# Second MLP products by Strassen's algorithm in three of four blocks, and a token order made at the output projection

## The chip, the cores and the metric

The kernel runs on one core of a Trainium2 chip (trn2). The metric is device time in microseconds for one execution, lower is better. The engines are named as in the profile: PE (TensorE matmul), PEld (its weight load), DVE (VectorE), ACT (ScalarE), POOL (GpSimd) and SP (SyncE, which issues most DMAs).

## The reference

A trunk of two residual layers over 1024 tokens of width 1024 in float32: neighbourhood attention and an MLP, then a gated DeltaNet and an MLP, and a last norm. The change is in the MLPs and in the output projection ahead of the first:

```python
def sq_relu_mlp(h, w1, w2):
    a = jax.nn.relu(h @ w1)
    return (a * a) @ w2

for i in range(DEPTH):          # DEPTH = 2, D_FF = 4096
    m, j = i % N_MIXERS, i // N_MIXERS
    if m == 0:
        h = h + neighbourhood_attention(rmsnorm(h, na_norm[j]), na_w_qkv[j], na_rpb[j], na_w_o[j])
    elif m == 1:
        h = h + gated_deltanet(rmsnorm(h, gdn_norm[j]), gdn_w_in[j], gdn_conv[j], ...)
    h = h + sq_relu_mlp(rmsnorm(h, mlp_norm[i]), mlp_w1[i], mlp_w2[i]).astype(h.dtype)
return rmsnorm(h, final_norm)
```

## The kernel before

Activations are held transposed: 8 row tiles d of 128 features by 1024 tokens, in two halves of 512 tokens. Each float32 operand is split into a high part (cast to fp32r on ACT, tiles `whi` and the like) and a low part (the difference, on DVE, `wlo`), and a product is three matmuls of 128x512: high x high, high x low, low x high (line 157).

`block` (line 91) runs an output projection and an MLP. `out_gather` (line 282) multiplies the attention result with `wo`, adds the residual `hr` at the eviction (line 305), takes squares and sums them over d on POOL (line 189), writes the residual to DRAM (`hs`), and gathers the seven right operands of Strassen's algorithm for the first products. The halves come in the order (d, 0), (d, 1); with `order` 2 the last four are (6, 0), (7, 0), (6, 1), (7, 1).

`mlp_first` (line 326) computes the hidden layer by Strassen's algorithm (Winograd's form): 16 column groups n, each with seven products of 12 matmuls (line 363). POOL forms the four left sums `s` (line 338) and two of the additions (line 348), ACT and DVE split the left operands (lines 353, 354), DVE evicts (line 348), scales and clips (line 343), ACT squares, and SP writes the result to DRAM (`hidden`).

`mlp_second` (line 400) multiplies the hidden layer with `w2` the plain way: four blocks b of 1024 hidden features; in each, for d and half, 24 matmuls into one PSUM bank, and one DVE addition to the residual `h` (line 431). The eight operand pairs of a block come from DRAM as tiles of 128x1024 and are split by `hidden_tile` (lines 394 to 396), those of the first block beside the last column group of `mlp_first` (`late`), those of the next beside the running one. `unspill` (line 709) loads the whole residual ahead of the first block. In the first MLP the last block reorders tokens from rows of the grid to the order that the next layer wants: with `reorder` the right operand of each matmul is read through a strided view, and the eviction goes to a new tile `hn` (line 428). After the last block `after` takes the norm of the result.

No planner sets the order of this part: each engine runs its instructions in the order that the tile framework lays down from the program, and tiles with a tag and `bufs` (three of `whi` and `wlo`, two of `mm`) say how far one engine may run ahead.

## Time and profile before

| | |
|---|---|
| median of 3 runs | 2812.89 us (2808.34 to 2814.01) |
| the profiled execution: its time | 2804.47 us |
| its span, granted TensorE clock | 2802.7 us, 0.985 |
| PE, DVE, ACT, POOL busy | 96%, 57%, 39%, 27% |
| first products of the first and second MLP, from and to | about 600 to 923 us, about 2090 to 2405 us |
| second products of the first and second MLP | about 925 to 1295 us, about 2410 to 2800 us |

Busy time is the time in which an engine works on an instruction. A matmul's end is modelled, so what one costs is read from how many start in a stretch. "Idle before" is the engine's idle time ahead of an instruction, with what ended it. The granted clock is a share of full speed.

### The profile page before, as it was taken

The numbers are of one execution on the slowest core, as the hardware profiler recorded it, in microseconds if no ns is written. First come the engines' busy times: TensorE is split into PE (matmuls) and PEld (weight loads), VectorE is DVE, ScalarE is ACT, GpSimd is POOL, SyncE is SP. The second block draws the span as 40 slices with busy tenths as digits, with TensorE's granted clock in tenths as the row PEclk, the third lists the DMA queues.
The fourth block names the chain that finished last, engine by engine and source line by source line (L and its number), as shares of the span: only waits on it lengthen the run. The fifth ranks groups of instructions, "written<-read, shape, count | busy, mean of one in ns | idle before, by whom it ended". The sixth has DMA issues, their size and how long they took to land. (4 is left out here: it accounts for less than half of the span.)

```text
span 2802.7 us, 39699 instructions
## 1 busy us (share of the span) xinstructions
PE 2704.1 (96%) x14460; PEld 2137.0 (76%) x14460; DVE 1603.9 (57%) x3137; ACT 1101.9 (39%) x2375; POOL 765.1 (27%) x951
## 2 busy tenths in 40 slices
PE   8999999999999999999998999999979999899998
PEld 6766666678888788887777887787858888788887
DVE  5155555665555532334778887787595555633333
ACT  5144444443333321123454555455353333411224
POOL 0111111154444000011334555543164444100001
PEclk9999999999999999999999999999989999999999
DMA  7212212333432532222221222214363433521323
GB/s 192 55 50 50 58 46 52 124 116 114 151 105 91 193 109 85 68 83 81 49 48 41 48 52 54 50 35 125 110 189 100 144 113 102 199 90 61 109 69 116
DMA packets 311667, 261.05 MB, mean 93 GB/s; under 512 B 78127, under 2 KB 256943, under 8 KB 311471
## 3 DMA queue, kind: packets, MB, share of 16 engines
q1 hardware_dynamic: 303054, 250.03, 29.8%
q0 software_dynamic: 3072, 8.39, 1.3%
q8 instruction: 114, 1.87, 0.3%
q10 hardware_dynamic: 5344, 0.09, 0.1%
q14 instruction: 83, 0.67, 0.1%
HBM read 183.56 MB, written 66.49 MB: 89 GB/s over the span
## 5 line engine op out<-in xcount | busy, mean ns | idle before, releaser
L157 PE MATMUL mm<-X,whi 128*128 128x512 f32 x1792 | 579.1, 399 | 5.9 <-ACT whi L133 5.0
L1371 PE MATMUL mm<-A,whi 128*128 128x512 f32 x1216 | 405.5, 414 | 1.1 <-DVE A L1371 1.1
L157 PEld LDWEIGHTS mm<-X,whi 128*128 128x128 f32 x1792 | 335.3, 188 | 87.6 <-issue 7.5
L157 PE MATMUL mm<-A,whi 128*128 128x512 f32 (+1 forms) x1104 | 350.5, 397 | 15.4 <-DVE hr L305 7.0
L157 PE MATMUL mm<-X,wlo 128*128 128x512 f32 x896 | 356.8, 399 | 0.0
L133 ACT CAST whi<-wraw 128x512 fp32r<-128x512 f32 (+1 forms) x210 | 128.0, 612 | 475.8 <-PE mm L157 427.1
L189 POOL TENSOR_TENSOR rs<-rs,r 128x512 f32<-128x512 f32 x55 | 77.5, 1410 | 797.2 <-ACT r L188 797.1
L157 PEld LDWEIGHTS mm<-A,whi 128*128 128x128 f32 x1104 | 207.2, 189 | 68.7 <-DVE hr L305 8.1
L1371 PEld LDWEIGHTS mm<-A,whi 128*128 128x128 f32 x1216 | 215.6, 191 | 41.5 <-DVE A L1371 1.9
L1371 PE MATMUL mm<-A,wlo 128*128 128x512 f32 x608 | 242.2, 398 | 0.0
L134 DVE TENSOR_TENSOR wlo<-wraw,whi 128x512 fp32r<-128x512 f32 (+1 forms) x210 | 155.1, 741 | 128.5 <-ACT whi L133 128.0
L431 DVE TENSOR_TENSOR h<-mm,h 128x512 f32<-128x512 f32 x111 | 76.7, 691 | 248.1 <-PE mm L157 247.6
L157 PE MATMUL mm<-A,wlo 128*128 128x512 f32 (+1 forms) x552 | 217.7, 395 | 0.1
L157 PEld LDWEIGHTS mm<-X,wlo 128*128 128x128 f32 x896 | 168.7, 188 | 37.6 <-issue 1.7
L344 ACT ACTIVATE r<-r 128x512 f32<-128x512 f32 x128 | 80.9, 632 | 234.2 <-DVE r L343 234.2
L354 DVE TENSOR_TENSOR wlo<-s,whi 128x512 fp32r<-128x512 f32 x128 | 118.8, 928 | 88.4 <-ACT whi L353 88.3
L1371 POOL TENSOR_TENSOR xt<-lp,xi 128x126 f32<-128x126 f32 (+22 forms) x248 | 106.0, 427 | 175.8 <-DMA lp<-dsc 157.0
L1371 DVE SCALAR_TENSOR_TENSOR X<-xp,cw,X 128x512 f32<-128x512 f32 x192 | 143.4, 788 | 1.7 <-ACT X L1371 1.0
L1371 PEld LDWEIGHTS mm<-A,wlo 128*128 128x128 f32 x608 | 115.5, 190 | 28.0
L157 PEld LDWEIGHTS mm<-A,wlo 128*128 128x128 f32 x552 | 104.7, 190 | 24.4 <-DVE wlo L134 0.5
L1371 POOL TENSOR_TENSOR xi<-xi,xt 128x126 f32<-128x126 f32 (+22 forms) x248 | 116.6, 470 | 19.4
L353 ACT CAST whi<-s 128x512 fp32r<-128x512 f32 x128 | 78.5, 613 | 76.2 <-PE mm L363 50.3
(331 smaller groups left out, 5346.5 us busy)
## 6 DMA issues: line engine op xcount, KB each, us to landing
wraw<-in_mlp_w_dram SPq DMA_DIRECT2D x148, 256.0 KB
quad<-in_mlp_w_dram SPq DMA_DIRECT2D x64, 512.0 KB
hidden<-r SPq DMA_DIRECT2D x128, 256.0 KB
X<-hidden SPq DMA_DIRECT2D x32, 512.0 KB
A<-hidden SPq DMA_DIRECT2D x32, 512.0 KB
wraw<-in_gdn_w_in_dram SPq DMA_DIRECT2D x64, 256.0 KB
wraw<-in_na_w_qkv_dram SPq DMA_DIRECT2D x32, 256.0 KB
hr<-hs SPq DMA_DIRECT2D x32, 256.0 KB
```

The source lines that it names most:

```text
L133: nc.scalar.copy(out=hi[:, :nk], in_=raw[:, :nk])
L134: nc.vector.tensor_tensor(out=lo[:, :nk], in0=raw[:, :nk], in1=hi[:, :nk].bitcast(FP32), op=ALU.subtract)
L157: nc.tensor.matmul(out=ps, lhsT=a, rhs=b, start=n == 0, stop=n == last)
L189: nc.gpsimd.tensor_tensor(out=st["acc", half], in0=st["acc", half], in1=sq, op=ALU.add)
L344: nc.scalar.activation(out=t, in_=t, func=AF.Square)
L353: nc.scalar.copy(out=hi, in_=left[j])
L354: nc.vector.tensor_tensor(out=lo, in0=left[j], in1=hi.bitcast(FP32), op=ALU.subtract)
L431: nc.vector.tensor_tensor(out=hv, in0=ps, in1=hv, op=ALU.add)
L1371: r = f(*args, **kw)
```

## The change

The second products of blocks 0 to 2 go by Strassen's algorithm too. A new class `Second` holds them: for each block b the seven products j in the order 1, 5, 2, 6, 3, 7, 4 (seven phases), and in each phase the four column groups q, each 12 matmuls into one of four PSUM banks. The right operands are quarter tiles of the hidden layer (128x512) and sums of them, the left ones quarters of `w2` and sums. POOL makes both kinds of sums in place (`combine`, `difference`) one to four phases ahead, ACT and DVE split the right operand of the next phase beside the running one (`split`), and the products are added up in the residual `h` and in three accumulators z, y, w. In the third block the eight whole tiles for the fourth block are loaded and split (`load`, `whole`), and POOL adds the accumulators to `h`. The first block's loads, splits and differences stand in the last column groups of `mlp_first` (`prepare`). The fourth block stays plain. `unspill` is gone; halves of the residual are loaded where they are first needed. Tokens of the first MLP are reordered at the eviction of the output projection: the sum goes through a strided view into a tile `now` of 128x1024, and square, spill and gather of both halves follow the second half; the last four halves there come as (6, 0), (6, 1), (7, 0), (7, 1).

```diff
-    def block(self, name, group, rest, spare, y, wo, gain, early, order, w1, w2, after, **how):
+    def block(self, name, group, rest, free, spare, y, wo, gain, early, order, w1, w2, after, moved=False, **how):
         st, other = {}, "X" if group == "A" else "A"
-        a = []
-
-        def late(j):
-            for f in {1: (0,), 5: (1, 2), 2: (3,), 6: (4, 5), 3: (6,), 7: (7,)}.get(j, ()):
-                a.append(self.hidden_tile(group, 0, f))
-
+        second = Second(self, group, other, rest, free, w2)
         with self.phase(name + "a", 1):
             get = self.operands(group, rest)
             with self.inner(name + "h"):
-                todo = self.out_gather(y, wo, gain, st, get, spare, early, order)
+                todo = self.out_gather(y, wo, gain, st, get, spare, early, order, moved)
             with self.inner(name + "w"):
-                self.mlp_first(st, w1, get, other, todo, late)
+                self.mlp_first(st, w1, get, other, todo, second, moved)
         with self.phase(name + "b"):
-            self.unspill()
-            self.mlp_second(a, (group, other), w2, after, **how)
+            a, h = second.blocks()
+            self.mlp_second(a, h, w2, after, **how)
...
-    def out_gather(self, y, wo, gain, st, get, spare, early, tail):
+    def out_gather(self, y, wo, gain, st, get, spare, early, tail, moved):
...
-        for n, (d, half) in enumerate(self.sequence(tail)):
+        for d, half in self.sequence(tail):
             if d not in w:
                 w = w if len(y) < 4 else {}
                 w[d] = self.weight(wo[:, d * P:(d + 1) * P])
-            hv = self.wk2.tile([P, HALF], FP32, tag="hr", name=self.uid("hr"), bufs=5)
-            nc.sync.dma_start(out=hv, in_=old[d][:, half * HALF:(half + 1) * HALF])
+            was = self.half("r") if moved else self.wk2.tile([P, HALF], FP32, tag="hr", name=self.uid("hr"), bufs=5)
+            nc.sync.dma_start(out=was, in_=old[d][:, half * HALF:(half + 1) * HALF])
             ps = self.product(w[d], y, half)
-            nc.vector.tensor_tensor(out=hv, in0=ps, in1=hv, op=ALU.add)
-            self.sumsq(d, half, hv, st)
-            self.spill(d, hv, half)
-            self.gather(d, half, hv, gain, get, raw, late)
-            if d // 2 < early:
-                for j in (5, 6, 7, 4):
-                    for f in late.pop(j, ()):
-                        f()
+            if moved:
+                if half == 0:
+                    now = self.wk2.tile([P, S], FP32, tag="hr", name=self.uid("hr"), bufs=2)
+                view = lambda t: t.rearrange("p (t r c) -> p t r c", r=16, c=8)
+                nc.vector.tensor_tensor(out=now.rearrange("p (r t c) -> p t r c", t=8, c=8)[:, 4 * half:4 * half + 4],
+                                        in0=view(ps), in1=view(was), op=ALU.add)
+                there = [(k, now[:, k * HALF:(k + 1) * HALF]) for k in range(2)] if half else []
+            else:
+                nc.vector.tensor_tensor(out=was, in0=ps, in1=was, op=ALU.add)
+                there = [(half, was)]
+            for k, hv in there:
+                self.sumsq(d, k, hv, st)
+                self.spill(d, hv, k)
+                self.gather(d, k, hv, gain, get, raw, late)
+                if d // 2 < early:
+                    for j in (5, 6, 7, 4):
+                        for f in late.pop(j, ()):
+                            f()
...
-                if n == nq - 1:
-                    late(j)
-
...
+                second.prepare(n - nq, j)
...
+    def combine(self, j, q):
+
+        tr = self.tr
+        if j == 5:
+            self.s[q] = tr.work("s1", [P, 4, P], 4)
+            self.less(self.s[q], self.left(7, q), self.left(4, q), ALU.add)
+        elif j == 6:
+            self.less(self.s[q], self.s[q], self.left(1, q))
+        elif j == 7:
+            self.less(self.left(7, q), self.left(7, q), self.left(1, q))
+        else:
+            self.less(self.left(2, q), self.left(2, q), self.s[q])
...
+    def prepare(self, n, j):
...
+        if j == 1:
+            for i in range(3):
+                self.split(0, 0, i)
+            self.load_b(0, "12", 0)
+        elif j == 5:
+            self.split(0, 0, 3)
+            self.load_b(0, "12", 1)
+        elif j == 2:
+            for i in range(4):
+                self.difference(5, i)
+            self.load_b(0, "21", 0)
+            self.load_w(0, 1, 0)
...
+    def beside(self, b, pos, q):
+
+        last = b == self.nb - 1
+        if pos < 6:
+            self.split(b, pos + 1, q)
+        elif not last:
+            self.split(b + 1, 0, q)
+        if pos == 0:
+            self.combine(5, q)
+        elif pos == 1:
+            self.combine(6, q)
+            self.difference(6, q)
+        elif pos == 2:
+            self.difference(7, q)
+        elif pos == 3:
+            self.combine(3, q)
+            self.difference(4, q)
+        elif pos == 4:
+            self.combine(7, q)
+        if not last:
+            if pos in (2, 3) and q % 2:
+                self.load_w(b + 1, 0, 2 * (pos - 2) + q // 2)
+            elif pos == 4:
+                self.load_b(b + 1, ("11", "22")[q // 2], q % 2)
+            elif pos == 5 and q % 2:
+                self.load_b(b + 1, "12", q // 2)
+            elif pos == 6:
+                self.difference(5, q)
+                self.load_w(b + 1, 1, q)
+                if q % 2:
+                    self.load_b(b + 1, "21", q // 2)
+        else:
+            n = 4 * pos + q
...
+            z, y, w = [self.sums[t, q] for t in "zyw"]
+            add = lambda out, x: self.less(out, out, x, ALU.add)
+            if pos == 5:
+                add(y, z)
+                add(self.h[2 * q, 1], y)
+            elif pos == 6:
+                add(self.h[2 * q + 1, 0], z)
+                add(self.h[2 * q + 1, 0], w)
+                add(w, y)
+                t = self.tr.work("h22", [P, HALF], 2)
+                self.tr.nc.sync.dma_start(out=t, in_=self.tr.hs[2 * q + 1][:, HALF:])
+                add(w, t)
+                self.h[2 * q + 1, 1] = w
...
+    def blocks(self):
...
+        for q in range(4):
+            fetch(2 * q, 0)
+        for b in range(self.nb):
+            self.block = b
+            for pos, j in enumerate(tr.ORDER):
+                for q in range(4):
+                    if b == 0 and pos in (2, 4):
+                        fetch(2 * q + pos // 4, 1 - pos // 4)
+                    hi, lo = [tr.sb.tile([P, 4, P], F32R, tag=tag, name=tr.uid(tag), bufs=3) for tag in ("whi", "wlo")]
+                    w = self.left(j, q)
+                    nc.scalar.copy(out=hi, in_=w)
+                    nc.vector.tensor_tensor(out=lo, in0=w, in1=hi.bitcast(FP32), op=ALU.subtract)
+                    ps = tr.ps.tile([P, HALF], FP32, tag="mm", name=tr.uid("mm"), bufs=2) if m % 2 else tr.bank("pq", [P, HALF], 2)
+                    m += 1
+                    for i in range(4):
+                        x = self.ops[j, i]
+                        for n, (u, v) in enumerate(((hi, 0), (hi, HALF), (lo, 0))):
+                            nc.tensor.matmul(out=ps, lhsT=u[:, i], rhs=x[:, v:v + HALF], start=i == 0 and n == 0, stop=i == 3 and n == 2)
+                    z, y, w = [self.sums[t, q] for t in "zyw"]
+                    if j in (1, 2):
+                        add(self.h[2 * q, 0], ps)
+                    elif j in (3, 4):
+                        add(self.h[2 * q, 1] if j == 3 else self.h[2 * q + 1, 0], ps)
+                    elif j == 6:
+                        add(z, ps)
+                    elif b:
+                        add({5: y, 7: w}[j], ps)
+                    else:
+                        nc.scalar.copy(out={5: y, 7: w}[j], in_=ps)
+                    if j == 1:
+                        if b:
+                            r = tr.half("r")
+                            nc.scalar.copy(out=r, in_=ps)
+                            self.less(z, z, r, ALU.add)
+                        else:
+                            nc.scalar.copy(out=z, in_=ps)
+                    self.beside(b, pos, q)
+        return self.ready, lambda d, half: self.h[d, half]
...
-    t.block("mlp0", "A", [f"X{i}" for i in range(7)], None, y, a["na_w_o"][0], g_m0, 3, 2, a["mlp_w1"][0], a["mlp_w2"][0], after, reorder=True)
+    t.block("mlp0", "A", [f"X{i}" for i in range(7)], [f"X{i}" for i in range(8, 14)], None, y, a["na_w_o"][0], g_m0, 3, 0,
+            a["mlp_w1"][0], a["mlp_w2"][0], after, moved=True)
```

How the order of instructions moves is shown at three places. DVE in the second block of the first MLP's second products, before (`mm` is a PSUM bank, `h2` to `h4` the residual, `wlo` a weight's low part):

```order
L134 TENSOR_TENSOR wlo_2153_8768<-wraw_2151_8765,whi_2152_8767 128x512
L431 TENSOR_TENSOR h2_2112_8540<-mm_2147_8733,h2_2112_8540 128x512
L134 TENSOR_TENSOR wlo_2160_8831<-wraw_2158_8828,whi_2159_8830 128x512
L431 TENSOR_TENSOR h3_2113_8542<-mm_2154_8771,h3_2113_8542 128x512
L134 TENSOR_TENSOR wlo_2163_8837<-wraw_2161_8834,whi_2162_8836 128x512
```

Between two weight splits stands one eviction, and a product of 24 matmuls belongs to each. After, in the third and fourth phase of the first block (`A0` to `A9`, `A2` are split right operands, `X4` and `X15` their sources, `A6` and `A7` the accumulator z, `mm` and `pq` PSUM banks):

```order
L242 TENSOR_TENSOR A0_2181_8856<-X4_2100_8476,A0_2181_8856 128x512
L242 TENSOR_TENSOR A8_2185_8879<-X4_2100_8476,A8_2185_8879 128x512
L242 TENSOR_TENSOR A1_2190_8904<-X15_2101_8479,A1_2190_8904 128x512
L1501 TENSOR_TENSOR h60_2119_8548<-mm_2175_8818,h60_2119_8548 128x512
L1514 TENSOR_TENSOR wlo_2188_8887<-s1_2134_8620,whi_2187_8886 128x512
L242 TENSOR_TENSOR A9_2194_8927<-X15_2101_8479,A9_2194_8927 128x512
L1501 TENSOR_TENSOR A6_2110_8536<-pq_2180_8842,A6_2110_8536 128x512
L1514 TENSOR_TENSOR wlo_2192_8910<-s1_2139_8644,whi_2191_8909 128x512
L1501 TENSOR_TENSOR A6_2110_8536<-mm_2184_8865,A6_2110_8536 128x512
L1514 TENSOR_TENSOR wlo_2198_8937<-A4_2087_8423,whi_2197_8936 128x512
L1501 TENSOR_TENSOR A7_2111_8537<-pq_2189_8890,A7_2111_8537 128x512
L1514 TENSOR_TENSOR wlo_2204_8964<-A12_2093_8447,whi_2203_8963 128x512
```

Twelve DVE operations now belong to four products of 12 matmuls, eight of them with both inputs in SBUF, and three operand splits stand together ahead of an eviction.

POOL from the end of the first MLP's first products, before (`r` is a hidden tile, `rs0` and `rs1` the sums of squares for the next layer's norm):

```order
L348 TENSOR_TENSOR r_2097_8466<-r_2097_8466,X15_2089_8437 128x512
L348 TENSOR_TENSOR r_2103_8495<-X14_2075_8381,X7_2069_8357 128x512
L189 TENSOR_TENSOR rs0_2368_10251<-rs0_2368_10251,r2_2383_10330 128x512
L189 TENSOR_TENSOR rs1_2372_10284<-rs1_2372_10284,r2_2386_10363 128x512
L189 TENSOR_TENSOR rs0_2368_10251<-rs0_2368_10251,r2_2397_10410 128x512
```

After, POOL's first operations for the second block (`s1` a weight sum from the two halves of the weights `X5` and `A4`, `X12`, `X13`, `X0` and `X1` quarter tiles of the hidden layer):

```order
L1359 TENSOR_TENSOR s1_2265_9258<-X5_2166_8786,A4_2242_9154 128x512
L1359 TENSOR_TENSOR X12_2201_8958<-X0_2228_9084,X12_2201_8958 128x512
L1359 TENSOR_TENSOR X5_2166_8786<-X5_2166_8786 128x4x128
L1359 TENSOR_TENSOR X12_2201_8958<-X0_2228_9084,X12_2201_8958 128x512
L1359 TENSOR_TENSOR X13_2207_8985<-X1_2237_9129,X13_2207_8985 128x512
L1359 TENSOR_TENSOR X0_2228_9084<-X0_2228_9084,X4_2213_9012 128x512
L1359 TENSOR_TENSOR s1_2271_9284<-X6_2177_8836,A12_2247_9178 128x512
L1359 TENSOR_TENSOR X0_2228_9084<-X0_2228_9084,X4_2213_9012 128x512
L1359 TENSOR_TENSOR X13_2207_8985<-X1_2237_9129,X13_2207_8985 128x512
```

POOL had nothing between the last addition of the first products and the sums of squares in the fourth block. Now 124 operations stand there in each MLP, and the first of a block (`s1`) stands ahead of the differences for that block's second phase (`X12`, `X13`).

POOL at the end of the first MLP's output projection, before (`raw` is a gathered operand, `rcol` the scales):

```order
L189 TENSOR_TENSOR rs0_1396_5193<-rs0_1396_5193,r2_1513_5790 128x512
L189 TENSOR_TENSOR rs1_1402_5230<-rs1_1402_5230,r2_1524_5839 128x512
L189 TENSOR_TENSOR rs1_1402_5230<-rs1_1402_5230,r2_1534_5885 128x512
L276 TENSOR_TENSOR raw_1503_5745<-raw_1503_5745,raw_1536_5892 128x512
L276 TENSOR_TENSOR raw_1514_5794<-raw_1514_5794,raw_1536_5892 128x512
L195 TENSOR_TENSOR rcol_1555_5959<-rcol_1555_5959,mhalf_70 128x4
```

After:

```order
L180 TENSOR_TENSOR rs1_1403_5231<-rs1_1403_5231,r2_1514_5785 128x512
L180 TENSOR_TENSOR rs0_1399_5222<-rs0_1399_5222,r2_1527_5860 128x512
L267 TENSOR_TENSOR raw_1512_5780<-raw_1512_5780,raw_1532_5876 128x512
L180 TENSOR_TENSOR rs1_1403_5231<-rs1_1403_5231,r2_1530_5869 128x512
L186 TENSOR_TENSOR rcol_1551_5943<-rcol_1551_5943,mhalf_70 128x4
L267 TENSOR_TENSOR raw_1528_5864<-raw_1528_5864,raw_1532_5876 128x512
```

The squares of tile 7 (`r2_1527`, `r2_1530`) are both added after the last product, with a difference between them.

## Rows read from the trace of the kernel before

**Rows 1.** The page's first part: busy time, share and instructions of each engine.

```profile
PE 2704.1 (96%) x14460; PEld 2137.0 (76%) x14460; DVE 1603.9 (57%) x3137; ACT 1101.9 (39%) x2375; POOL 765.1 (27%) x951
```

**Rows 2.** Stretches: length, busy time (instructions) of PE, PEld, DVE, ACT, POOL; clock, DMA share, GB/s.

```profile
620.00:900.00 280.00, 280.00 (x1205) 225.26 (x1204) 161.10 (x228) 107.57 (x187) 128.26 (x88) 1.00 0.36 115
965.00:1215.00 250.00, 250.00 (x1074) 201.43 (x1073) 78.57 (x106) 45.14 (x63) 0.00 (x0) 1.00 0.26 81
1222.00:1282.00 60.00, 60.00 (x266) 49.53 (x265) 25.00 (x37) 22.44 (x36) 14.63 (x11) 1.00 0.34 105
```

**Rows 3.** Groups, 640 to 900 us (last: 960 to 1200): count, busy, mean ns, idle before.

```profile
L354 DVE TENSOR_TENSOR wlo<-s,whi 128x512 fp32r<-128x512 f32 x55 | 51.0, 927 | 37.9 <-ACT whi L353 37.9
L354 DVE TENSOR_TENSOR wlo<-quad,whi 128x512 fp32r<-128x512 f32 x39 | 26.7, 685 | 7.9 <-ACT whi L353 7.9
L348 DVE TENSOR_TENSOR r<-pq,X 128x512 f32<-128x512 f32 x26 | 17.8, 686 | 19.5 <-PE pq L363 19.5
...
L353 ACT CAST whi<-s 128x512 fp32r<-128x512 f32 x54 | 33.1, 613 | 31.0 <-PE mm L363 23.7 <-PE p L363 7.3
...
L338 POOL TENSOR_TENSOR s<-quad 128x512 f32<-128x512 f32 x14 | 23.5, 1676 | 16.8 <-DVE wlo L354 16.8
L338 POOL TENSOR_TENSOR s<-s,quad 128x512 f32<-128x512 f32 x14 | 18.1, 1295 | 47.4 <-DVE wlo L354 47.4
...
L396 DVE TENSOR_TENSOR A<-A,A 128x1024 fp32r<-128x1024 f32 x8 | 9.7, 1222 | 4.4 <-ACT A L395 4.4
```

**Rows 4.** Timeline in the first MLP's first products: start, length, engine, instruction.

```profile
750.97 1.29 POOL L348 TENSOR_TENSOR r<-X,X 128x512 f32<-128x512 f32 x1 [1.41 <-DVE X L348]
751.50 1.31 DVE L354 TENSOR_TENSOR wlo<-s,whi 128x512 fp32r<-128x512 f32 x1 [0.61 <-ACT whi L353]
...
741.53 0.69 DVE L348 TENSOR_TENSOR r<-mm,X 128x512 f32<-128x512 f32 x1 [1.27 <-PE mm L363]
742.14 0.68 DVE L354 TENSOR_TENSOR wlo<-s,whi 128x512 fp32r<-128x512 f32 x1
...
612.79 1.25 POOL L338 TENSOR_TENSOR s<-quad,quad 128x512 f32<-128x512 f32 x1
614.01 1.26 POOL L338 TENSOR_TENSOR s<-quad 128x512 f32<-128x512 f32 x1
```

**Rows 5.** Timeline where both engines have work queued, second MLP's output projection.

```profile
2081.57 1.78 DVE L251 TENSOR_TENSOR A<-raw,A 128x512 fp32r<-128x512 f32 x1
2083.27 1.78 DVE L254 SCALAR_TENSOR_TENSOR X<-hr,g_m,X 128x512 fp32r<-128x512 f32 x1
...
2081.05 1.75 POOL L189 TENSOR_TENSOR rs<-rs,r 128x512 f32<-128x512 f32 x1
2082.75 1.75 POOL L276 TENSOR_TENSOR A<-A,A 128x512 f32<-128x512 f32 x1
```

**Rows 6.** Stretches at the change from first to second products, both MLPs.

```profile
920.00:940.00 20.00, 16.56 (x63) 12.46 (x62) 19.90 (x23) 14.09 (x18) 3.23 (x2) 0.91 0.57 201
940.00:960.00 20.00, 18.32 (x79) 14.41 (x78) 9.27 (x12) 3.53 (x5) 0.00 (x0) 1.00 0.88 295
2400.00:2420.00 20.00, 15.60 (x53) 11.57 (x53) 17.39 (x20) 15.06 (x20) 2.32 (x2) 0.83 0.54 180
2420.00:2440.00 20.00, 17.70 (x76) 13.91 (x74) 10.26 (x12) 3.86 (x6) 0.90 (x1) 1.00 0.99 347
2440.00:2460.00 20.00, 19.50 (x78) 15.70 (x79) 9.74 (x13) 5.56 (x8) 0.00 (x0) 0.91 0.30 94
```

**Rows 7.** PE's waits for the sums of squares: total us, times, longest.

```profile
PE pa L203 <- POOL rs L189: 6.2, 2, 5.4
```

**Rows 8.** Stretches in the gated DeltaNet, columns as in rows 2.

```profile
1360.00:1380.00 20.00, 16.89 (x74) 13.49 (x74) 16.65 (x42) 10.08 (x29) 6.18 (x8) 0.83 0.14 27
1440.00:1460.00 20.00, 18.38 (x119) 15.83 (x118) 16.09 (x45) 13.18 (x39) 2.77 (x6) 1.00 0.07 11
```

**Rows 9.** A stretch at the end of the second MLP's output projection.

```profile
2080.00:2100.00 20.00, 12.38 (x50) 10.28 (x49) 18.59 (x19) 9.00 (x16) 18.01 (x12) 0.67 0.27 84
```

More of the change, by code (lines that the diff above doesn't have):

```diff
@@ L142, in pair, with product @@
         return self.slot(f"{group}{i}", F32R), self.slot(f"{group}{8 + i}", F32R)
-    def product(self, w, xs, half, order=None, sl=None, ps=None):
+    def product(self, w, xs, half, sl=None):
         nc = self.nc
-        ps = ps or self.ps.tile([P, HALF], FP32, tag="mm", name=self.uid("mm"), bufs=2)
+        ps = self.ps.tile([P, HALF], FP32, tag="mm", name=self.uid("mm"), bufs=2)
         sl = sl or slice(half * HALF, (half + 1) * HALF)
@@ L151, in product @@
         for (whi, wlo), (xhi, xlo) in zip(w, xs):
-            if order is None:
-                hi, lo = xhi[:, sl], xlo[:, sl]
-            else:
-                hi, lo = order(xhi)[:, 8 * half:8 * half + 8], order(xlo)[:, 8 * half:8 * half + 8]
-            for a, b in ((whi, hi), (whi, lo), (wlo, hi)):
-                nc.tensor.matmul(out=ps, lhsT=a, rhs=b, start=n == 0, stop=n == last)
+            for a, b in ((whi, xhi), (whi, xlo), (wlo, xhi)):
+                nc.tensor.matmul(out=ps, lhsT=a, rhs=b[:, sl], start=n == 0, stop=n == last)
                 n += 1
@@ L386, in mlp_first, with mlp_second @@
                     finish(add(self.half("r2"), ps, p1), 1, 0)
-                if n == nq - 1:
-                    late(j)
-    def hidden_tile(self, group, b, f):
+                second.prepare(n - nq, j)
+    def mlp_second(self, a, h, w2, after, tail=2, cut=False):
         nc = self.nc
-        hi, lo = self.pair(group, f)
-        nc.sync.dma_start(out=lo.bitcast(FP32), in_=self.hidden[b * ND + f])
-        nc.scalar.copy(out=hi, in_=lo.bitcast(FP32))
-        nc.vector.tensor_tensor(out=lo, in0=lo.bitcast(FP32), in1=hi.bitcast(FP32), op=ALU.subtract)
-        return hi, lo
@@ new lines, in mlp_second @@
+        w = [None, None]
+        for d, half in self.sequence(tail):
+            if w[0] != d:
+                w = [d, self.weight(w2[w2.shape[0] - D:, d * P:(d + 1) * P])]
+            hv = h(d, half)
+            if cut and (d, half) == (ND - 1, 1):
+                for part in range(2):
+                    sl = slice(part * 256, part * 256 + 256)
+                    ps = self.product(w[1], a, half, sl=slice(HALF + sl.start, HALF + sl.stop))
+                    nc.vector.tensor_tensor(out=hv[:, sl], in0=ps, in1=hv[:, sl], op=ALU.add)
+                    after(d, half, hv[:, sl], part)
+                continue
+            ps = self.product(w[1], a, half)
+            nc.vector.tensor_tensor(out=hv, in0=ps, in1=hv, op=ALU.add)
+            after(d, half, hv)
@@ L689, in na @@
         return y + [y7]
-    def out_proj(self, y, wo, after, tail=2):
-        nc = self.nc
-        w = {}
-        for i, (d, half) in enumerate(self.sequence(tail)):
-            if d not in w:
-                w = w if len(y) < 4 else {}
-                w[d] = self.weight(wo[:, d * P:(d + 1) * P])
-            ps = self.product(w[d], y, half, ps=self.bank("pa", [P, HALF]) if i == 2 else None)
-            hv = self.h[d][:, half * HALF:(half + 1) * HALF]
-            nc.vector.tensor_tensor(out=hv, in0=ps, in1=hv, op=ALU.add)
-            after(d, half, hv)
     def spill(self, d, hv, half=None):
@@ L707, in spill @@
         self.nc.sync.dma_start(out=dst, in_=hv)
-    def unspill(self):
-        self.h = []
-        for d in range(ND):
-            h = self.work(f"h{d}")
-            self.nc.sync.dma_start(out=h, in_=self.hs[d])
-            self.h.append(h)
     def gdn_consts(self, conv, onorm):
```

133 lines of the change are left out of this document (95 added, 38 removed).

## The prediction

> **What bounds the kernel now.** I read the busy shares first: TensorE (PE) is busy for 96% of the span, VectorE (DVE) for 57%, GpSimd (POOL) for 27% [rows 1]. So the end is set by PE's instruction stream, and an edit pays by the matmuls it removes, as long as the others can still feed PE. Then I read the stretches of the MLPs. In the first products 1205 matmuls start in 280 us, 0.2324 us each; in the second products 1074 in 250 us, 0.2328 us; both at granted clock 1.00 [rows 2]. PE does not wait there. In the second products DVE works 79 of 250 us and POOL not at all; in the first products, already Strassen, DVE works 161 of 280 us and POOL 128 [rows 2]. The change turns the first picture into something heavier than the second, so the question is what DVE and POOL cost each other.
>
> They do cost each other. The same DVE subtraction (wlo) takes 685 ns beside no POOL work and 927 ns on average where POOL writes its input; POOL's own addition takes 1295 or 1676 ns [rows 3]. One case is plain: POOL's addition starts at 750.97 and lasts 1.29 us, and the DVE subtraction that starts at 751.50 ends at 752.81, 0.55 us after POOL's end. Undisturbed, DVE starts an operation each 0.61 us (741.53, 742.14) and POOL each 1.22 (612.79, 614.01) [rows 4]. With both queued they go in lockstep: DVE starts at 2081.57 and 2083.27, POOL at 2081.05 and 2082.75, so 1.70 us buy one of each, about 1.25 for POOL and 0.45 for DVE [rows 5]. DVE's additions from PSUM have one input in SBUF; they keep 686 ns [rows 3].
>
> **The change: matmuls.** Each Strassen block has 7 x 4 products of 12 matmuls, 336 where 384 stood. Three blocks in two MLPs: 288 fewer, x 0.2324 = **-66.9 us**. All of it lies on PE's path. Against it, the last block of the first MLP loses its strided right operand: 266 matmuls in 60 us there, 0.2256 each, against 0.2328 for a plain one [rows 2]; 384 x 0.0072 = **+2.8**.
>
> **Change of stage.** Between first and second products PE now starts 63 + 79 matmuls in 40 us and, in the second MLP, 53 + 76 + 78 in 60 us [rows 6]; at 0.2326 there is room for 172 and 258, so 30 and 51 are missing: 7.0 and 11.9 us. DVE is busy 19.9 of 20 us there and the DMA engines up to 0.99: eight tiles of 128x1024 are loaded and split, and the residual is loaded. After the change PE needs only four 128x512 halves for its first product, split beside the last seven products, and the residual only at eviction. The last column group carries 8 more splits, though (8 x 0.61 on DVE), so I leave 3 to 4 us at each: **-12**, between -19 (seamless) and 0.
>
> **DVE and POOL in the Strassen blocks.** A product takes PE 12 x 0.2324 = 2.79 us, a phase of four 11.16, a block 78.1. Per phase DVE splits four weights and four operands (8 operations with two inputs in SBUF) and evicts four times: 12 x 0.61 = 7.3 us, 84 x 0.61 = 51.2 per block. POOL gets 32, 36 and 40 operations in the three blocks up to the sixth phase, x 1.25 = 40 to 50 us. Alone, each fits. In lockstep the eight two-input operations of a phase take 8 x 1.70 = 13.6 us, the evictions hidden under POOL: +2.44 per phase that holds eight POOL operations. The code lets DVE run two products ahead (three buffers of whi and wlo), which swallows some 3 us per block. Upper bound per MLP: 108 / 8 x 2.44 = 33, less 3 x 3, plus some 5 for the eight 128x1024 splits (1.22 us each [rows 3]) in the third block: 29, so 58 for both. Lower bound 0: the first products run both engines and lose nothing [rows 2]. The excess there is (927 - 685) ns x 55 = 13 us over some 80 POOL operations (six groups of 13 or 14, two of them in [rows 3]), 0.16 each, with DVE 58% busy; here DVE is at 66% before any wait, and POOL's order gives it a queue through most of a block. I take **+25**, under the middle of the bounds, since the near row is the first products.
>
> A page of the Trainium skill speaks for a harder price. The SBUF page ("SBUF — State Buffer", section "Who interferes with whom") says that a DVE instruction with two SBUF inputs and a GpSimd instruction that reads SBUF exclude each other, and its section "SBUF: two separate sides" that the holder keeps the port for the whole instruction. By that a pair would take 1.25 + 0.69 = 1.94 and the time would be the 2854 of the fifth rival; the rows show 1.70, so the two overlap by about 0.2 us, and I keep 1.70 [rows 5].
>
> **ACT, DMA and queues at nothing.** ACT gets two casts of 0.61 us per product [rows 3] and at times a copy, under 1.9 of 2.79 us. Weights and hidden tiles of a block are 8 MB in 78 us, near 105 GB/s where 347 was seen [rows 6]. SyncE issues them in order; the eviction waits for no load after the first four residual halves.
>
> **Output projection of the first MLP.** The eviction gathers both halves of a row tile after the second, and the order of the last four products changes. So after the last matmul POOL must do both squares' sums and one difference before the second row of scales, where one sum stood: 2 more at 1.25 to 1.7. PE already waits up to 5.4 us there [rows 7]. **+3**, between 0 and 6.
>
> **Third to fourth block.** 16 POOL additions (20 us) follow the last phase and run beside the fourth block, whose evictions need them 11 us and more later; its first splits meet POOL. **+4** for both MLPs, 0 to 8.
>
> **Sum.** -66.9 + 2.8 - 12 + 25 + 3 + 4 = -44.1. The profiled execution took 2804.5 us, so 2760; it lies 8.4 under the median of 2812.9, and against that the sum gives **2769**.
>
> **The rivals.** (1) POOL's work falls into DVE's gaps as in the first products, contention 3 instead of 25: 2747. For it: the pitch in those [rows 2]; against it: half as many POOL operations again per product. (2) Full lockstep, 58: 2802. For it: POOL's order stands ready one block ahead; against it: POOL waits for DVE before most of its operations in the first products [rows 3]. (3) Data late: POOL's first operation for a block needs the second half of the weights, whose load waits for the last phase's splits, and the operands of the next phase stand behind it. If that costs 10 us at each of four changes of block: +40, 2809, no difference. The load would have to be 20 us late; some 5 MB in 33 us speak against it. (4) **Slower, by the clock.** In lockstep PE works 11.16 of 13.6 us, 82%. A slice in which it was busy 16.9 of 20 us had granted clock 0.83, one with 18.4 had 1.00 [rows 8], and 0.67 stands where DVE and POOL were both nearly full and PE started 50 matmuls in 20 us [rows 9]. Lockstep covers 2 x 108 / 8 = 27 phases. At a mean of 0.75 a phase takes 14.9, +3.7 x 27 = +100 in place of 25: +31, 2844. It decides from a mean of 0.81 in those phases (13.7 us). Against it: no long idle stretch, only short ones. (5) The port held through all of both instructions: 8 x 1.94 = 15.5, +4.4 x 27 = 118, less 18, plus 10: 110 for 25, 2854. The Trainium skill's SBUF page above has it as its rule. Against it stand [rows 5].
>
> **How the numbers follow.** Forecast 0.48, with its own range 2751 to 2787 (contention 10 to 40, the other terms between their bounds); rival 1 0.25, 2 0.12, 3 0.05, 4 0.08, 5 0.02. About 0.2% (5.6 us) can be told from no change. Faster: 0.48 + 0.25 + 0.12 = 0.85; same 0.05; slower 0.10. The range 2740 to 2812 takes in rivals 1 and 2 and leaves out 4, 5 and half of 3.
>
> **What would show it.** 288 fewer 128x512 matmuls; in the new blocks some 12 matmuls per 2.8 to 3.1 us with the clock at 1.00; wlo means of 0.8 to 1.1 us there, POOL means of 1.4 to 1.6; DVE over 80% busy; no 20 us with fewer than 75 matmuls at the change to the second products. I am wrong if PE waits there for DMA or for POOL's weight combinations rather than for wlo, if the clock in the blocks is under 0.9, or if wlo stays at 0.69.

## The result

The changed kernel takes 2820.07 us (2811.99 to 2823.8, 12 runs) where the kernel before takes 2808.68 beside it: a ratio of 1.004, interval 1.0027 to 1.0053, which is 8 to 15 us slower. Forecast were 2769 and a range of 2740 to 2812. The two profiled spans, 2820.3 and 2802.7 us, differ by 17.6, because the profiled execution of the kernel before lies 4 us under its median and that of the changed kernel 2 us over.

The page after, its line on busy time (engine, us, share, instructions; before: [rows 1]):

```profile
PE 2662.4 (94%) x14172; PEld 2086.9 (74%) x14172; DVE 1883.8 (67%) x3381; ACT 1205.2 (43%) x2603; POOL 1169.1 (41%) x1207
```

288 matmuls are gone, as the change says. But PE now waits in the new blocks (L1520). Its waits there, over the whole run: total us, times, longest us:

```profile
PE pq L1520 <- DVE wlo L1514: 24.6, 20, 2.2
PE pq L1520 <- ACT whi L1513: 21.1, 4, 6.4
PE mm L1520 <- DVE wlo L1514: 11.7, 18, 2.0
PE mm L1520 <- ACT whi L1513: 4.0, 2, 2.0
```

These are 61 us, 36 for low parts (`wlo`) and 25 for high parts (`whi`). Stretches of 20 us in the first MLP's second products (columns as in [rows 2]; 86 to 88 matmuls have room; before: [rows 6]):

```profile
920.00:940.00 20.00, 16.81 (x70) 12.67 (x69) 15.75 (x18) 6.95 (x12) 14.20 (x10) 1.00 0.79 260
940.00:960.00 20.00, 15.66 (x64) 11.42 (x62) 17.89 (x14) 10.04 (x19) 20.00 (x14) 1.00 0.83 281
1040.00:1060.00 20.00, 12.64 (x42) 9.36 (x43) 15.17 (x13) 8.43 (x15) 20.00 (x15) 0.74 0.00 1
1120.00:1140.00 20.00, 13.62 (x50) 10.23 (x49) 12.61 (x12) 6.53 (x12) 19.77 (x15) 0.86 0.00 0
```

POOL is full in the last three of these stretches and works 14 of 20 us in the first; in the last two the DMA engines do nothing and DVE itself waits. The groups of DVE and POOL from 930 to 1200 us show why (busy us, mean ns | idle before; before: [rows 3]):

```profile
L242 DVE TENSOR_TENSOR A<-X,A 128x512 fp32r<-128x512 f32 x76 | 95.0, 1276 | 16.6 <-ACT A L241 16.3
L1514 DVE TENSOR_TENSOR wlo<-s,whi 128x512 fp32r<-128x512 f32 x24 | 26.1, 1089 | 0.0
L1501 DVE TENSOR_TENSOR h<-pq,h 128x512 f32<-128x512 f32 x22 | 15.0, 683 | 5.4 <-PE pq L1520 4.5 <-DMA h<-hs 0.9
L1359 POOL TENSOR_TENSOR X<-X,X 128x512 f32<-128x512 f32 x44 | 70.1, 1617 | 0.2
L1359 POOL TENSOR_TENSOR s<-X,A 128x512 f32<-128x512 f32 x12 | 19.9, 1664 | 66.3 <-DMA A<-in_mlp_w_dram 35.4 <-DVE A L242 30.9
```

The subtractions that read two tiles from SBUF take 1.1 to 1.3 us in these groups where 0.685 was the undisturbed price; the evictions, with one operand in PSUM, keep 0.683. POOL's sums take 1.6 to 1.7 for 1.25. And POOL stood idle for 66 us ahead of two weight sums `s`.

From the start of each phase's first matmul to that of the next, a phase of four products (48 matmuls) takes 11.2 us undisturbed. What the phases of the changed kernel take over that is 79.8 us in both MLPs (39.8 and 40.0; the very first phase, whose start is the change of stage, is not counted, and takes 14.2 and 13.9 us), 56 of it idle PE and the rest slower matmuls; the granted clock over the blocks is 0.96. The expectations of the experiments speak of 82 us and of phases of 22.3, 20.4, 21.9 and 19.7 us. There each phase was taken to start one product too early: PE begins the stage with four matmuls of one product, runs another and then ends the first, and this had been counted as three products. By position in the block, with the experiments beside it:

| us over 11.2, both MLPs | 1st | 2nd | 3rd | 4th | 5th | 6th | 7th | all |
|---|---|---|---|---|---|---|---|---|
| changed kernel | 10.3 | 47.7 | 13.9 | 0.6 | 1.4 | 5.9 | 0.0 | 79.8 |
| e1 program order on POOL | 0.0 | 10.0 | 18.9 | 37.3 | 3.6 | 3.1 | 0.0 | 72.8 |
| e2 last products swapped | 8.5 | 25.8 | 9.3 | 0.5 | 0.9 | 3.5 | 12.9 | 61.3 |
| e6 sums without readers | 1.3 | 26.6 | 0.0 | 15.9 | 1.9 | 6.1 | 2.8 | 54.6 |
| e9 low parts as copies | 0.0 | 22.4 | 1.7 | 0.7 | 0.0 | 0.0 | 0.0 | 24.8 |

The worst phases are the second ones of blocks two and three, 22.1, 20.4, 22.2 and 20.0 us. One of them, on POOL (with the idle time ahead), ACT, DVE, and PE at its start, its longest wait and its end:

```profile
973.34 6.90 POOL L1359 TENSOR_TENSOR A<-A,s 128x512 f32<-128x512 f32 x4
1011.16 1.72 POOL L1359 TENSOR_TENSOR s<-X,A 128x512 f32<-128x512 f32 x1 [30.92 <-DVE A L242]
1012.85 1.75 POOL L1359 TENSOR_TENSOR X<-X,X 128x512 f32<-128x512 f32 x1
...
1020.46 1.74 POOL L1359 TENSOR_TENSOR s<-X,A 128x512 f32<-128x512 f32 x1
1022.16 6.85 POOL L1359 TENSOR_TENSOR X<-X,X 128x512 f32<-128x512 f32 x4
...
1034.09 1.73 POOL L1359 TENSOR_TENSOR s<-X,A 128x512 f32<-128x512 f32 x1
...
1042.41 2.48 POOL L1359 TENSOR_TENSOR A<-A,r 128x512 f32<-128x512 f32 x2
```

```profile
1032.90 0.62 ACT L241 CAST A<-X 128x512 fp32r<-128x512 f32 x1
1043.70 0.59 ACT L1535 COPY r<-pq 128x512 f32<-128x512 f32 x1 [10.17 <-POOL A L1359]
...
1045.22 0.62 ACT L1513 CAST whi<-s 128x512 fp32r<-128x512 f32 x1
```

```profile
1044.83 1.82 DVE L242 TENSOR_TENSOR A<-X,A 128x512 fp32r<-128x512 f32 x1 [8.46 <-ACT A L241]
```

```profile
1033.76 0.63 PE L1520 MATMUL pq<-A,whi 128*128 128x512 f32 x2
...
1045.89 1.22 PE L1520 MATMUL pq<-A,whi 128*128 128x512 f32 x2 [6.37 <-ACT whi L1513]
...
1055.89 0.63 PE L1520 MATMUL pq<-A,whi 128*128 128x512 f32 x2
```

POOL ends one block's sums at 980.2, stands 31 us behind the next block's first `s` (its input is a load that comes into slots read until the last phase; the row names a split of DVE that ended at the same time), and then has that block's sums to do at 1.7 us each, those of later phases in among the four `s`. Its additions to the accumulator z (`A<-A,r`) come behind these, at 1042.4. ACT copies the first phase's products for z into `r`, a tile of two buffers (`half`), so its third copy waits 10.2 us until POOL has added the first. Behind that copy, in ACT's order, stand the splits of the third phase and the `whi` for which PE waits 6.4 us. The operands of the third phase themselves are plain quarters, no sums; the 8.5 us that DVE waits are the same wait passed on. In the third block this copy waits 8.9 us, and so again in the second MLP: these four make up PE's 21.1 us for `whi`.

So there were two suspects. **Theory A, lateness:** POOL's order and the late load. **Theory B, contention:** each POOL sum slows DVE, and DVE each sum, at any place.

### The profile page after: what moved, and what is told of

Read it like the earlier page. It is cut to its first block, busy times and chain, and to the rows that moved or that the text cites. A ratio compares the mean times of both kernels' runs of the same rounds, so it can differ in the third digit from the quotient of the medians.

```text
span 2820.3 us, 40024 instructions
## 1 busy us (share of the span) xinstructions
PE 2662.4 (94%) x14172; PEld 2086.9 (74%) x14172; DVE 1883.8 (67%) x3381; ACT 1205.2 (43%) x2603; POOL 1169.1 (41%) x1207
## 5 line engine op out<-in xcount | busy, mean ns | idle before, releaser
L148 PE MATMUL mm<-X,whi 128*128 128x512 f32 x1024 | 338.7, 403 | 0.7 <-ACT X L657 0.7
L1555 PEld LDWEIGHTS mm<-A,whi 128*128 128x128 f32 x1216 | 216.0, 192 | 41.4 <-DVE A L1555 1.9
L148 PEld LDWEIGHTS mm<-X,whi 128*128 128x128 f32 x1024 | 191.1, 189 | 47.4 <-issue 7.5
L148 PE MATMUL mm<-X,wlo 128*128 128x512 f32 x512 | 206.0, 403 | 0.0
L1555 PEld LDWEIGHTS mm<-A,wlo 128*128 128x128 f32 x608 | 115.8, 191 | 28.1
L242 DVE TENSOR_TENSOR X<-A,X 128x512 fp32r<-128x512 f32 x93 | 112.4, 1233 | 20.1 <-ACT X L241 19.5
L148 PE MATMUL mm<-A,whi 128*128 128x512 f32 (+1 forms) x336 | 109.8, 403 | 12.9 <-DVE hr L304 6.3
L1520 PE MATMUL pq<-X,whi 128*128 128x512 f32 x336 | 110.9, 412 | 10.6 <-ACT whi L1513 10.6
L1520 PE MATMUL pq<-A,whi 128*128 128x512 f32 x336 | 110.0, 409 | 11.5 <-ACT whi L1513 10.6
L242 DVE TENSOR_TENSOR A<-X,A 128x512 fp32r<-128x512 f32 x84 | 101.7, 1235 | 20.2 <-ACT A L241 19.6
```

The costliest lines, as they stand in the source:

```text
L148: nc.tensor.matmul(out=ps, lhsT=a, rhs=b[:, sl], start=n == 0, stop=n == last)
L242: nc.vector.tensor_tensor(out=t[:, HALF:], in0=src, in1=t[:, :HALF].bitcast(FP32), op=ALU.subtract)
L1520: nc.tensor.matmul(out=ps, lhsT=u[:, i], rhs=x[:, v:v + HALF], start=i == 0 and n == 0, stop=i == 3 and n == 2)
L1555: r = f(*args, **kw)
```

## The experiments

Times of one chip are compared by their ratio to the kernel before on it, which took 2804.3 to 2804.8 us in these runs; by the ratio the changed kernel would take about 2816 there. The expectations of e1 to e4 are on the scale on which it takes 2820.

**e1: POOL in program order.**

```diff
-            a, h = second.blocks()
+            with self.tc.manual_schedule(engines={mybir.EngineType.Pool}):
+                a, h = second.blocks()
```

> GpSimd runs the sums of the Strassen blocks in the order in which the program writes them; nothing else is edited. In the changed kernel the phases of the new blocks (11.2 us undisturbed) cost 82 us more than that in all, 39 to 40 us of it in the second phase of the second and third block of each MLP (22.3, 20.4, 21.9, 19.7 us). There POOL stood 31 us behind the first weight sum of the block (s1, which waits for a load) and then put sums that are needed two to four phases later ahead of the other three s1. Theory A (lateness by POOL's order): with the sums in the order of need those four phases fall to 12 to 14 us, 30 to 36 us are gained, 2784 to 2790 where the changed kernel takes 2820. Theory B (the DVE and POOL in lockstep, 1.70 us a pair, whatever the order): the number of sums is the same, so no more than 6 us change, 2814 to 2826.

Measured: 2812.42 us, ratio 1.0028 (1.0015 to 1.0042), 2816.5 on the scale of the expectation, where B had put it. But the phases say that A's part is real too: the second ones lose 10.0 us for 47.7, and ACT's copies to `r` no longer wait for POOL. The gain went into a new wait in the fourth phase of the third block (24.6 and 26.3 us). ACT, from 1143 us, and PE's waits there (920 to 1215 us):

```profile
1143.89 0.62 ACT L1514 CAST whi<-s 128x512 fp32r<-128x512 f32 x1 [2.87 <-PE pq L1521]
1160.16 1.04 ACT L1484 CAST X<-X 128x1024 fp32r<-128x1024 f32 x1 [15.66 <-POOL X L1360]
```

```profile
PE pq L1521 <- ACT whi L1514: 12.7, 3, 10.9
```

The cast of a whole tile for the fourth block stands in ACT's order ahead of casts that PE needs now, and waits for a load into a slot that POOL's operand sums now hold until 1156 us (the row names the POOL operation that ended just as the load landed). Order alone moves the loss.

**e2: the last two products of a block change places**, so the second half of the weights comes one phase earlier.

```diff
+    ORDER = (1, 5, 2, 6, 3, 4, 7)
...
-            elif pos == 5 and q % 2:
-                self.load_b(b + 1, "12", q // 2)
+            elif pos == 5:
+                self.load_w(b + 1, 1, q)
+                if q % 2:
+                    self.load_b(b + 1, "12", q // 2)
             elif pos == 6:
                 self.difference(5, q)
-                self.load_w(b + 1, 1, q)
```

> The last two products of a Strassen block change places (1, 5, 2, 6, 3, 4, 7), so the second half of the weights (k2) is last read one phase, 11 us, earlier and the next block's is loaded one phase earlier. POOL's order is left to the framework. Theory A, in its narrow form (only the late load matters): POOL's block of sums starts some 11 us earlier and the four phases of 20 to 22 us fall to 12 to 14: 2784 to 2792. If it is the order among the sums and not the load, part remains: 2795 to 2810. Theory B (lockstep alone): 2814 to 2826.

Measured: 2792.07, ratio 0.9961 (0.9947 to 0.9975). On the scale of the expectation this is 2798: in the range where part of the loss remains, and outside both the narrow form's and B's. POOL's block starts 14 us earlier:

```profile
997.44 1.77 POOL L1360 TENSOR_TENSOR s<-X,A 128x512 f32<-128x512 f32 x1 [18.37 <-DVE A L242]
```

The phases lose 18 us less (61.3 for 79.8) and the time falls by 22 to 24; the other 61 stay. What went is mostly the wait behind ACT's copy: in the first MLP PE waits 2.2 us for `whi` where the changed kernel has 12.6, and 20.1 for `wlo` where it has 17.7 (920 to 1215 us).

**e3: no sums on POOL.**

```diff
     def difference(self, j, i):
+        return
...
     def combine(self, j, q):
+        return
...
-        if j in (5, 6):
-            return self.s[q]
-        t = self.k[self.block, 1 if j in (1, 7) else 2, q]
+        t = self.k[self.block, 1 if j in (1, 7, 5) else 2, q]
```

> Left out: the sums that POOL makes for the Strassen blocks, of weights and of operands; the products take plain quarters in their place, so the matmuls, the splits, the loads and the evictions stay. POOL keeps the additions to z and the 16 at the end of each third block. Both theories: all of POOL's share goes, the phases are 11.2 us but for the change of stage and the third block's end: 70 to 80 us less than the changed kernel, 2740 to 2750. A third reading (DVE, ACT or DMA are the limit by themselves): 2780 or more.

Measured: 2728.9, ratio 0.9732 (0.9715 to 0.9748), 87 us under the changed kernel, and below the 2740 to 2750 that both theories gave. All 192 sums together cost that; POOL keeps 64 additions, 16 to z and 24 at the end of each third block. The phases lose 1.1 us in all, so loads, splits and evictions cost nothing, at the change of stage either (compare [rows 6] and the stretches above; the first line is the page's):

```profile
PE 2628.6 (97%) x14172; PEld 2075.5 (76%) x14172; DVE 1757.0 (65%) x3381; ACT 1208.1 (44%) x2603; POOL 861.0 (32%) x1015
920.00:940.00 20.00, 20.00 (x87) 16.01 (x86) 12.47 (x20) 7.81 (x14) 2.90 (x2) 1.00 0.98 314
940.00:960.00 20.00, 20.00 (x87) 16.11 (x86) 12.17 (x20) 11.11 (x22) 0.00 (x0) 1.00 0.80 276
```

**e4: all of POOL's work in these blocks on DVE.**

```diff
-        self.tr.nc.gpsimd.tensor_tensor(out=out, in0=x, in1=y, op=op)
+        self.tr.nc.vector.tensor_tensor(out=out, in0=x, in1=y, op=op)
```

> All sums of the Strassen blocks and the additions to z and at the end go to DVE; POOL has none of them. DVE's work per block is then 84 operations plus 32 to 40 sums, at 0.61 to 0.69 us each 71 to 86 us where PE needs 78.4. Theory B (the pair at 1.70 us is the cost): a pair costs DVE 1.22 to 1.38 in place of 1.70, the excess of 82 us falls to some 20 to 40: 2760 to 2780. Theory A (lateness, which DVE's order may have too): a sum that waits for the load now stands in DVE's own queue ahead of splits and evictions, so 2800 or slower.

Measured: 2745.72, ratio 0.9792 (0.9774 to 0.981), 2750 on the scale of the expectation: below what B allowed, and against A. The page's line, and two groups from 930 to 1200 us:

```profile
PE 2642.9 (96%) x14172; PEld 2082.0 (76%) x14172; DVE 1874.1 (68%) x3637; ACT 1209.6 (44%) x2603; POOL 766.5 (28%) x951
```

```profile
L242 DVE TENSOR_TENSOR A<-X,A 128x512 fp32r<-128x512 f32 x77 | 52.0, 685 | 0.5 <-ACT A L241 0.3
L1359 DVE TENSOR_TENSOR X<-X,X 128x512 f32<-128x512 f32 x44 | 29.8, 684 | 0.0
```

DVE does 256 instructions more than in the changed kernel and is busy 10 us less. In numbers: 192 sums on POOL raise DVE's busy time from 1757.0 (e3) to 1883.8, 0.66 us each; the same sum on DVE itself takes 0.684. POOL took nothing off DVE.

What e4 still loses lies at the end of the third block, where DVE also has the whole tiles:

```profile
1160.00:1180.00 20.00, 14.85 (x54) 10.84 (x53) 19.61 (x29) 4.49 (x6) 0.00 (x0) 0.84 0.21 74
```

**e5: as e4, the additions at the end back on POOL**, and z by DVE from PSUM.

```diff
-            add = lambda out, x: self.less(out, out, x, ALU.add)
+            add = lambda out, x: self.less(out, out, x, ALU.add, self.tr.nc.gpsimd)
...
-                            r = tr.half("r")
-                            nc.scalar.copy(out=r, in_=ps)
-                            self.less(z, z, r, ALU.add)
+                            add(z, ps)
```

> As the run with all sums on DVE, but the 24 additions at the end of each third block stay on POOL, and z takes its product by a DVE addition from PSUM without ACT's copy. With everything on DVE the third block's end starts only 54 and 52 matmuls in one stretch of 20 us in each MLP (86 to 88 have room), beside DVE at 19.6 and 19.1 of 20 us: 32 and 34 missing, 15 us in all. If that is DVE's number of operations there, 8 to 14 us come back: 2732 to 2740 on the same scale (2745.7 with all on DVE). If POOL's additions at the end cost DVE as much as they take off it, the time stays within 4 us.

Measured: 2744.78, ratio 0.9782 (0.9756 to 0.9808), the same as e4 within the intervals. The missing matmuls mostly moved to an earlier stretch (the phases lose 15.6 us where e4's lose 22.4, the times differ by 1):

```profile
1140.00:1160.00 20.00, 16.91 (x69) 12.11 (x68) 20.00 (x24) 8.22 (x13) 7.35 (x5) 1.00 0.21 67
1160.00:1180.00 20.00, 20.00 (x87) 16.02 (x87) 16.94 (x20) 6.78 (x9) 10.71 (x7) 1.00 0.26 80
```

The 48 additions on POOL bring nothing that the time shows: DVE is full beside them. Both versions are about 60 us faster than the kernel before.

**e6: sums without readers.** As e3, but POOL makes 184 sums that nothing waits for.

```diff
+    def spare(self, q):
+        t = self.ops[self.now, q].bitcast(FP32)
+        self.less(self.scratch[q % 2], t[:, :HALF], t[:, HALF:], ALU.add)
...
     def combine(self, j, q):
+        self.spare(q)
+        return
```

> As the run without POOL's sums (2728.9 us), but in the place of each of them (but the first four of a stage) POOL adds the two halves of an operand tile of the running phase into a tile that nobody reads: 184 additions of 128x512 with two inputs in SBUF, no consumer, no load to wait for. What they cost is the shared way to SBUF alone, without lateness. Theory B (lockstep is most of the 82 us): 40 us or more above 2729, POOL at 1.5 to 1.74 us each, phases with eight POOL additions at 13 to 15 us. Theory A (lateness is most): under 15 us above 2729.

Measured: 2786.79, ratio 0.9935 (0.9911 to 0.996): 58 us above e3, as B has it (its profiled execution is the slowest of four, 7 us above their median). No data can be late here for want of a sum, and yet (930 to 1200 us):

```profile
L242 DVE TENSOR_TENSOR A<-X,A 128x512 fp32r<-128x512 f32 x76 | 96.3, 1294 | 8.0 <-issue 7.3 <-ACT A L241 0.3
L1359 POOL TENSOR_TENSOR sc<-A 128x512 f32<-128x512 f32 x92 | 150.3, 1658 | 63.2 <-DVE A L242 62.4
```

In the first MLP PE waits 18.4 us for `wlo`, as in the changed kernel (17.7), but 1.5 for `whi` in place of 12.6. Nor do the extra sums hold up the splits whose tiles they read: ACT's casts into these tiles have 12.5 us of idle time ahead of them, 10.7 of it behind PE.

**e7: low parts on ACT.** The other side: POOL as in the changed kernel, DVE without its subtractions there.

```diff
-                    nc.vector.tensor_tensor(out=lo, in0=w, in1=hi.bitcast(FP32), op=ALU.subtract)
+                    nc.scalar.copy(out=lo, in_=w)
...
-        self.tr.halves(t, self.b[...])
+        src = self.b[...]
+        for part in range(2):
+            self.tr.nc.scalar.copy(out=t[:, part * HALF:(part + 1) * HALF], in_=src)
```

> In the Strassen blocks the low parts (wlo and those of the operands) are made as copies on ACT where DVE subtracted; the result is not the reference's. POOL's sums, their order, their inputs and the loads are those of the changed kernel; DVE keeps there only additions from PSUM and the eight whole tiles. Theory B: POOL's sums take 1.25 to 1.3 us each, the phases fall near 11.2 us except where ACT (four operations of 0.6 us per product of 2.8) falls behind: 2735 to 2765. Theory A: POOL still starts its block's sums behind the late load and the second phases of blocks two and three stay at 17 us or more: 2775 to 2800.

Measured: 2730.6, ratio 0.9737 (0.9713 to 0.976), 2 us from e3, slightly under B's range; A falls as a cause by itself. DVE also has less to do here, but e3 and e4 show that its own work delays no second phase. POOL, 930 to 1200 us, its start of the second block, and a stretch that holds that block's second phase:

```profile
L1361 POOL TENSOR_TENSOR X<-X,X 128x512 f32<-128x512 f32 x44 | 56.6, 1308 | 65.5 <-ACT A L1357 34.6 <-DMA A<-in_mlp_w_dram 30.7
```

```profile
995.80 2.66 POOL L1361 TENSOR_TENSOR X<-X,X 128x512 f32<-128x512 f32 x2 [30.69 <-DMA A<-in_mlp_w_dram]
```

```profile
1020.00:1040.00 20.00, 18.95 (x81) 14.66 (x80) 4.15 (x6) 16.81 (x33) 20.00 (x17) 1.00 0.13 46
```

POOL waits 31 us as in the changed kernel. At 1.31 us a sum it still comes nearly in time: the second phases of blocks two and three take 12.8 to 13.1 us, 7 us over in all.

**e8: the projection's part alone**, with plain second products.

```diff
-    t.block(..., g_m0, 3, 2, a["mlp_w1"][0], a["mlp_w2"][0], after, reorder=True)
+    t.block(..., g_m0, 3, 0, a["mlp_w1"][0], a["mlp_w2"][0], after, moved=True)
```

> The kernel before with one part of the change: the tokens are reordered at the eviction of the first MLP's output projection; the second products stay plain and lose the strided operand and the tile hn. By the prediction's terms +2.8 us (384 matmuls at 0.2328 for 0.2256) and +3 us (0 to 6) at the projection's end: 2.8 to 8.8 us slower than before, ratio 1.001 to 1.003. If the projection's new order is free, 1.001; if the strided operand's price was not real, 1.000 to 1.002.

Measured: 2807.98, ratio 1.0008 (0.9995 to 1.002), some 2 us, no difference that this can tell from none. The projection's end (before, then e8) and the last block:

```profile
560.00:620.00 60.00, 56.11 (x242) 45.72 (x241) 41.16 (x48) 27.38 (x46) 32.76 (x22) 0.92 0.42 126
560.00:620.00 60.00, 56.10 (x242) 44.95 (x240) 39.74 (x44) 27.11 (x47) 30.79 (x22) 0.93 0.41 122
1222.00:1282.00 60.00, 60.00 (x259) 48.35 (x258) 23.33 (x34) 20.99 (x34) 13.42 (x10) 1.00 0.30 95
```

259 matmuls where 266 stood [rows 2]: the strided operand's price is real, 384 x (60/259 - 60/266) = 2.3 us. The projection's end starts 242 matmuls in those 60 us, as many as the kernel before in the same stretch: free.

**e9: low parts as copies on DVE**, one input in SBUF for two.

```diff
-                    nc.vector.tensor_tensor(out=lo, in0=w, in1=hi.bitcast(FP32), op=ALU.subtract)
+                    nc.vector.tensor_copy(out=lo, in_=w)
...
+        self.tr.nc.vector.tensor_copy(out=t[:, HALF:], in_=src)
```

> In the Strassen blocks DVE makes the low parts as plain copies of one SBUF tile (weights and operands alike), where the changed kernel subtracts two; the result is not the reference's. ACT's casts, POOL's sums with their order and inputs, and the loads are those of the changed kernel. If it is two inputs in SBUF on both engines that shut each other out: POOL's sums at 1.25 to 1.35 us, phases near 11.2, 2730 to 2745 as with the low parts on ACT. If any DVE operation from SBUF to SBUF does it: POOL at 1.5 us and more, 2770 to 2820.

Measured: 2749.28, ratio 0.98 (0.9761 to 0.9839), between the two readings. Copies collide as well, at a lower price for POOL (930 to 1200 us; the shortest of these copies take 0.41 us):

```profile
L1357 DVE CAST A<-X 128x512 fp32r<-128x512 f32 x76 | 77.8, 1051 | 2.7 <-PE mm L1522 2.0 <-ACT A L1356 0.3
L1361 POOL TENSOR_TENSOR X<-X,X 128x512 f32<-128x512 f32 x44 | 62.4, 1440 | 59.8 <-ACT A L1356 59.7
```

So "two inputs" is not the whole condition. The Trainium skill's SBUF page ("SBUF — State Buffer", section "Who interferes with whom") has copies and casts of DVE among the operations that can take the way it shares with GpSimd; this run agrees with that. It also gives a scale for lateness: at 1.31 us a sum (e7) the second phases lose 7 us in all, at 1.44 (e9) 22, at 1.62 to 1.66 (the changed kernel) 48. ACT's copy to `r` waits for POOL by the same scale: 4.0 to 4.5 us in e7, 7.5 to 8.9 in e9, 8.9 to 10.2 in the changed kernel.

## Why the prediction was wrong

By its own terms, in us:

| term | predicted | found |
|---|---|---|
| 288 matmuls | -66.9 | 14460 to 14172, as predicted |
| strided operand | +2.8 | +2.3 (e8) |
| projection's end | +3 | about 0 (e8) |
| change of stage | -12 | there to be had (e3), but with POOL's sums beside it 70 + 64 matmuls start where 63 + 79 did [rows 6], and the first phases lose 3.0 and 2.7 |
| DVE and POOL in the blocks; third to fourth block | +25 and +4 | +79.8 in the phases |
| ACT and queues | 0 | PE waits 21 us for `whi` behind ACT's copy, within the 79.8 |

-66.9 + 2.3 + 79.8 is 15.2, and the profiled spans differ by 17.6, so the remaining terms come to some 2 us together: the change of stage gave nothing back. The term of the projection's end started from a misread row: the wait of 5.4 us in [rows 7] is that of the second MLP's projection; in the first MLP's the longest wait for the scales is 1.7 us.

**The step that failed is the +25**, twice, and with it ACT and the queues, put at nothing.

First its size. The mechanism was right and its row too: 1.70 us a pair [rows 5]. Of the means asked for in the prediction's last part that of wlo came (1.0 to 1.1), POOL's lie above theirs (1.6 to 1.7 for 1.4 to 1.6). The upper bound of 58 is about what contention alone costs: e6 measures 58. That they agree so closely is luck, since the bound counts 216 operations of POOL and e6 makes 184 such sums. I went under the middle of the bounds because the first products showed an excess of only 0.16 us per POOL operation [rows 2, 3]. That row was the wrong neighbour. In the first products POOL waits for DVE before most of its operations [rows 3] and PE loses nothing; here POOL has a block of sums in its queue and works without a gap, and each sum costs DVE 0.66 us (e3 against the changed kernel).

Second, the rivals were priced as if one excluded the other. "Full lockstep" (+58) and "data late" (+40) both came: of the 87 us that the sums cost (e3) contention makes 58 by e6, and some 29 are left, of which the earlier load gives back 22 to 24 in e2. Lateness had 0.05, on the ground that the load would have to be 20 us late. The ground was a wrong question: POOL did wait 31 us, and e7 shows that this wait costs 7 us while a sum takes 1.3. It was the slow sums after the wait that ran past PE's need. Contention makes the lateness; a chance for the second had to hang on the first.

Third, ACT's term was worked out from its time, two casts and at times a copy in under 1.9 of 2.79 us. That came: ACT works 111 of the 278 us of the first MLP's new blocks. What it left out is the order. ACT's copy to `r` waits for POOL, up to 10.2 us, and the `whi` that PE needs stands behind it. This path is read from the trace; a run with more buffers for `r`, which would show what it is worth by itself, was not made.

**The rivals besides.** The clock (rival 4) did sink, to 0.74 and 0.86 in the worst stretches, but the mean over the blocks is 0.96, where the rival needed 0.81 in 27 of the 42 phases, and it is low behind a wait: two matmuls take 1.22 us after the wait of 6.4 us, 0.63 at the phase's start. Slower matmuls make some 23 of the 80 us, idle PE 56. Rival 5, by which a pair takes 1.94 us, doesn't hold to the letter: POOL's own pitch in the changed kernel is 1.70 (1011.16 to 1012.85, and 6.85 for four). The Trainium skill's SBUF page ("SBUF — State Buffer", section "SBUF: two separate sides") has the holder keep the way for the whole instruction; these rows show some 0.2 us less.

Of the signs that the prediction named, the stretches under 75 matmuls at the change of stage are there (70 and 64). The others came in part: the clock is under 0.9 in the worst stretches alone, and PE waits 36 of its 61 us for wlo, as forecast, but 25 for whi, the longest of them behind POOL's additions. What stays open is how e1's program order would do with ACT's order mended; it was not tried.

## What to carry to other kernels

Before giving work to GpSimd "because it is idle", look in the trace for what one of its operations does to a VectorE operation beside it; if a sum costs the other engine as much time as doing the sum there, keep it there: e4 is the same change with one word altered and takes 0.979 of the time before, where the change as made takes 1.004. Take the contention from a row in which both engines have a queue, not from one where one waits for the other. And when two rivals share a cause, price them together: an engine slowed by contention also catches up more slowly after each wait. An engine with time to spare, like ACT here, can still hold up another by its order: look at what stands behind each instruction that has to wait.

## What the runs showed of the hardware

In these blocks GpSimd's 128x512 addition costs VectorE 0.66 us of busy time (the changed kernel against e3), against 0.684 for the same addition on VectorE (e4); evictions from PSUM beside it keep 0.68. A VectorE copy from SBUF collides too: 1.05 us on average for the operands' copies (the shortest 0.41), and POOL's sums beside it 1.44, against 1.31 where VectorE has no operation of that kind (e7). ACT's casts and copies cost POOL little or nothing (e7: 1.31 us a sum beside ACT at 16.8 of 20 us, 1.25 undisturbed [rows 4]).
